# Mixture-of-experts tail of a decoder block: groups gathered in one burst a pair later, 33 weight blocks asked ahead, the spill loop amid pair 14

## The chip, the cores and the metric

The kernel runs on one core of one Trainium2 chip, in one launch. Times are device microseconds (us). The core has TensorE (PE: matmuls, and PEld: weight loads of the array), VectorE (DVE), ScalarE (ACT), GpSimd (POOL) and SyncE (SP), which here issues DMAs. Tiles live in SBUF; matmuls write PSUM, of which the kernel uses eight banks.

## The reference

One layer for 512 tokens of width 1024, in float32: a gated linear attention and a block-sparse softmax attention in parallel, cross-attention into 256 memory tokens, and a mixture of experts (MoE). The change touches the MoE and what follows it:

```python
# top-1 of 4 groups, top-2 of 8 SwiGLU experts in the group: 1024 assignments over 32 experts
hid = silu(xb @ w_gate[e]) * (xb @ w_up[e])      # (.., 1024) -> (.., 512)
out[tok] += (hid @ w_down[e]) * w                # (.., 512) -> (.., 1024)
return rmsnorm(x + moe(rmsnorm(x, g_moe)), g_final)
```

Each of the 32 experts has 6.29 MB of float32 weights, 201 MB together, and all of them are read.

## The kernel before

**Stages.** Up to about 500 us run the two attentions, the cross-attention and the router. The rest, which is about half of the time, is the MoE in 16 pairs of experts (`for p in range(NP)`), and then the final norm and the stores.

**Slots.** Every expert has 64 slots (`CAP`). A token's two assignments become integer codes (expert number times 512, plus rank in the expert). A group is four experts, that is two pairs: `group_hots` (L1187) compares the codes with the group's 256 slots on VectorE and leaves a one-hot tile `oh`; `gather` (L1195) multiplies the tokens' high and low halves with it on TensorE, eight steps of eight matmuls of 256 columns, and ScalarE copies each step's PSUM bank into `xT`. Group 0 is gathered during the routing (`c_gather`, L1037), the last part of it just ahead of pair 0.

**One pair.** `gate_up` (L1219): eight steps `k` of eight PE instructions into two PSUM banks `gu`; `hidden` (L1225): Silu on ScalarE, product on VectorE; `hidden_t` (L1232): transposes on TensorE and a copy on ScalarE; `down` (L1240): four steps `ft` into `y_ps`; `rows_hilo` splits that. While ScalarE and VectorE make the hidden values, TensorE runs fillers: steps of the generator `comb`, which puts the pair before back on its tokens (`c_ps`, added to `x` on VectorE), and steps of `gat`, the gather of the next group. Before, a group's gather starts in the even pair and takes four steps there and four in the odd pair after it, for pairs two and three further on; its `oh` is made at the end of the odd pair ahead.

**Weights.** `load_pairs` (L953) lists the loads of 512 KB: for each pair 16 of gate and up (L940, in four rounds of four), then 8 of down (L946). So load 24 p is the first of pair p. `eload(n)` (L966) asks for loads up to number n on SP's queue. Each takes a tile of the pool `bp`, of `NB` = 48 tiles, and waits on SP until the tile's last reader is done; tiles come back in the order in which they were let go. The pool also holds `x` (4 tiles), the tokens' halves `xrh` and `xrl` (8), the broadcast weights `wts` (1), `xT` (2 for each group that is alive) and `oh` (1). `DEPTH` = 30 says how many loads beyond the pair's first are asked for at its start; `D0` says it for pair 0. The DMA completions are counted on eight semaphores, and a load waits until the one eight before it has landed.

**Codes spread.** `c_bcast` (L1066) turns codes and weights so that every partition holds all of them: four steps, each of four transposes on TensorE and a copy on ScalarE, for two rows of codes and two of weights. `slot_rows` (L1205) reads them on VectorE for each pair. Before, the four steps stand in pair 0, at k = 2 to 5.

**Spill loop.** Assignments beyond an expert's 64 slots would be done by `overflow` (L1265), a loop with a run-time count; with these inputs the count is zero. Its entry reads the count into a register of each engine (L1266), and all engines meet twice (L1268). Before, it stands ahead of pair 15. `elimit` holds the loads back at 368 until it is passed (`12 * (NE - 2) + SPILL_AT`).

**End.** `finish` (L1385) scales and stores each 128-token tile in two halves of 256 KB (L1388, L1390), all eight stores on SP's queue.

Of the kernel before, what the change touches and what calls it, by code (L numbers as in the profile page):

```python
# [21 lines left out]
P = 128  # L22
T = 512
# [3 lines left out]
NE = 32  # L27
CAP = 64
# [42 lines left out]
def block_kernel(ctx, tc, x, mem, g_mem, rel_bias, g_mix, w_in, w_alpha_up, b_alpha, g_gla_head, w_proj_gla,  # L71
# [3 lines left out]
    nc = tc.nc  # L75
# [25 lines left out]
    def ps(name, shape, parts=P):  # L101
        return pp.tile([parts] + list(shape), F32, tag="p", name=name)
# [54 lines left out]
    def drain(*gens):  # L157
        for g in gens:
            for _ in g:
                pass  # L160
# [775 lines left out]
    def load_gate_up(e, to=None):  # L936

        for i, (q, w) in enumerate((q, w) for q in range(4) for w in (w_exp_gate, w_exp_up)):
            b = to[i % len(to)] if to else blk("we", [2, 512])
            SY.dma_start(b, wexp(w, e, 2 * q, 2 * q + 2))  # L940
            yield b
# [6 lines left out]


    blocks = [[] for _ in range(NE)]  # L950
    eloads, elimit = [0], [12 * (NE - 2) + SPILL_AT]

    def load_pairs():  # L953
        for p in range(NE // 2):
# [77 lines left out]
    def c_gather_part(t, kk, q):  # L1032
        for a in range(2):
            mm(g0[kk][:, a, :], (xrh, xrl)[q][t][:, tcol(2 * kk + a)], oh[:, t, :], t == 0 and a == 0 and q == 0,
               t == NT - 1 and q == 1, skip_group_check=True)
# [19 lines left out]
    def c_weights():  # L1055
        V.tensor_tensor(ge, gl, bc(gm, [NT, 4]), op=ALU.subtract)
        V.tensor_tensor(ex, m2, m1, op=ALU.subtract)
        S.activation(ge, ge, AF.Exp)
        S.activation(ex, ex, AF.Exp)
        V.tensor_reduce(gs, ge, axis=AX.X, op=ALU.add)  # L1060
        V.scalar_tensor_tensor(den, ex, 1.0, gs, op0=ALU.add, op1=ALU.mult)
        V.reciprocal(wts[:, :, 0:1], den)
        V.tensor_tensor(wts[:, :, 1:2], wts[:, :, 0:1], ex, op=ALU.mult)
        V.tensor_scalar(sid, e512, pslot, None, op0=ALU.add)
# [76 lines left out]
    c_low(NT - 1)  # L1141
    for kk in range(KD // 2):
        c_gather_part(NT - 1, kk, 0)
    c_weights()
    c_gather(NT - 1)
    S.activation(small("warm", [1]), neghalf[:, 0:1], AF.Silu)
# [45 lines left out]
            tile_hots(oh, rel, t, 4 * CAP)  # L1192
        return oh

    def gather(oh, xT, ns):  # L1195

        for k in range(KD):
            o = ps("g_ps", [ns])
            for t in range(NT):
                for q, src in enumerate((xrh, xrl)):  # L1200
                    mm(o, src[t][:, tcol(k)], oh[:, t, :], t == 0 and q == 0, t == NT - 1 and q == 1)
            S.activation(xT[k], o, AF.Copy, scale=gfeat[:, k:k + 1])
            yield
# [21 lines left out]
    def hidden(gu, ws, n=P, hid=None):  # L1225
        hid = (med("hid", [4, P]) if hid is None else hid)[0:n]
        row = hid.rearrange("p a b -> p (a b)")
        S.activation(row, gu[0][0:n], AF.Silu)  # L1228
        V.scalar_tensor_tensor(row, row, ws[:, 0:1], gu[1][0:n], op0=ALU.mult, op1=ALU.mult)  # L1229
        return hid  # L1230

    def hidden_t(hid, n=P):  # L1232
        t_ps = ps("ht_ps", [4, n])
        for a in range(4):
            PE.transpose(t_ps[:, a, :], hid[:, a, :], ident[0:n, 0:n])  # L1235
        hid_t = med("hid_t", [4, n])
        S.activation(hid_t, t_ps, AF.Copy)
        return hid_t
# [13 lines left out]
        for i in range(2):  # L1252
            mm(o, ot[:, tcol(t)], y[i], first and i == 0, i == 1)

    def combine(ot, ys):

        for t in range(NT):
            for c, y in ys.items():
                o = ps("c_ps", [512])
                product(o, ot, t, y)  # L1260
                xs = x_sb[t][:, 512 * c:512 * c + 512]
                V.tensor_tensor(xs, o, xs, op=ALU.add)  # L1262
                yield t, c

    def overflow(xi, xb):  # L1265
        n_extra = nc.values_load(xi[0:1, 0:1], min_val=0, max_val=NX - 1,  # L1266
                                 skip_runtime_bounds_check_because="2 T assignments fill fewer than NX whole blocks")
        with tc.For_i(0, n_extra, 1, iteration_sync='staggered') as i:  # L1268
            e = nc.sync.value_load(xi[0:1, bass.ds(i + 1, 1)], min_val=0, max_val=NE - 1)
            base = small("base", [1])  # L1270
            V.tensor_copy(base, xb[:, bass.ds(i, 1)])
            rel = small("relx", [NT, 2])
            V.tensor_scalar(rel, code, base, None, op0=ALU.subtract)
            codes = small("codes", [1])
            V.tensor_tensor(codes, pslot, base, op=ALU.add)
            take, take2 = cut(blk("loop", [D])), cut(blk("loop2", [D]))
            oh, part, oa = blk("oh", [NT, CAP], F32R), take([CAP]), take([T])
            xT, hid = take2([KD, CAP]), take2([4, P])
            xT = [xT[:, k, :] for k in range(KD)]
            for t in range(NT):  # L1280
                tile_hots(oh, rel, t, CAP, part)
            drain(gather(oh, xT, CAP))
            ot, ws = slot_rows(codes[0:CAP], CAP, oa)
            to = [blk("we", [2, 512]) for q in range(4)]
            gu, load = [ps("gu_ps", [512]) for q in range(2)], load_gate_up(bass.ds(e, 1), to)
            for j in range(4):
                w = list(islice(load, 2))
                for k in (2 * j, 2 * j + 1):
                    gate_up(gu, k, xT[k:k + 1], [{2 * j + q: w[q] for q in range(2)}])
            hid_t = hidden_t(hidden(gu, ws, CAP, hid), CAP)  # L1290
            y_ps, load = [ps("y_ps", [512]) for c in range(2)], load_down(bass.ds(e, 1), to)
            for ft in range(4):
                down(y_ps, hid_t, ft, [{8 + ft: next(load)}])
            parts = med("yh", [512], F32R), med("yl", [512], F32R)
            for c in range(2):
                drain(combine(ot, {c: rows_hilo(y_ps[c], CAP, parts)}))

    NP = NE // 2
    bcast, slot, spill = c_bcast(), None, spill_list()
    comb, gat = iter(()), iter(())  # L1300
    xT_next = None
    for p in range(NP):
        w = blocks[2 * p:2 * p + 2]
        used = 24 * p
        if p == NP - 1:
            eload(elimit[0])
            overflow(*spilled)
            elimit[0] = 12 * NE
        eload(used + D0[0] if p == 0 else used + DEPTH)
        if p % 2 == 0 and p:  # L1310
            xT = xT_next
        gu = [ps("gu_ps", [512]) for q in range(2)]
        s0 = (p % 2) * P
        for k in range(KD):
            gate_up(gu, k, [xT[k][:, s0 + CAP * i:s0 + CAP * i + CAP] for i in range(2)], w)
            if k % 2:
                eload(D0[1 + k // 2] if p == 0 else used + DEPTH + 2 * (k + 1))
            if p == 0 and k >= BC_AT:
                next(bcast, None)
                if k == BC_AT + 3:  # L1320
                    slot = slot_rows(sid[:, 0:1])
                    oh_next = group_hots(1)
        if p % 2 == 0 and p + 2 < NP:
            xT_next = rows2("xT", KD, 4 * CAP)
            gat = gather(oh_next, xT_next, 4 * CAP)
        if p == NP - 1:
            gf = blk("gf", [D])
            SY.dma_start(gf, bcast_rows(g_final, D))
        hid = hidden(gu, slot[1])
        gs = 4 if p + 2 < NP else 0  # L1330
        steps(gat, min(gs, 1))
        steps(comb, 2 if gs else 4)
        hid_t = hidden_t(hid)
        for i in range(3):
            steps(gat, min(gs, 1))
            steps(comb, 2)
        drain(comb)
        ot = slot[0]
        if p + 1 < NP:
            slot = slot_rows(sid[:, 2 * p + 2:2 * p + 3])  # L1340
        if p % 2 and p + 3 < NP:
            oh_next = group_hots((p + 3) // 2)
        if p >= 2:
            next(spill, None)
        y_ps = [ps("y_ps", [512]) for c in range(2)]
        if p == NP - 1:
            break
        for ft in range(4):
            down(y_ps, hid_t, ft, w)
            eload(used + DEPTH + 16 + 2 * (ft + 1))  # L1350
        ys = {c: rows_hilo(y_ps[c]) for c in range(2)}
        comb = combine(ot, ys)


# [30 lines left out]
    def finish(t, r):  # L1385
        o = blk("xo", [512])
        V.scalar_tensor_tensor(o, x_half(t, 1), r, gf[:, 512:1024], op0=ALU.mult, op1=ALU.mult)  # L1387
        SY.dma_start(out[tcol(t), 512:1024], o)  # L1388
        S.activation(xg[t], xg[t], AF.Copy, scale=r)
        SY.dma_start(out[tcol(t), 0:512], xg[t])  # L1390

    part = [last_products(c) for c in range(2)]
    for ft in range(4):
# [15 lines left out]
            finish(t - 1, r[t - 1])  # L1409


SPILL_AT = 8
MEM_AT, WOS = (0, 1), {5: 4, 6: 4}
LATE = [], [], range(4)
BC_AT = 2
# [2 lines left out]
QW = (0, 3, 4, 4)  # L1418
NB = 48
WARM = (14, 12)  # L1420
DEPTH = 30
D0 = 34, 37, 41, 44, 47
AHEAD, SAHEAD = 4, 2
FILL = (4, 3), (5, 3), (5, 4), (5, 4)
MANUAL = None
# [28 lines left out]
```

## Time and profile before

| | us |
|---|---|
| median of 3 runs (985.02 to 985.25) | 985.21 |
| the profiled execution | 985.1 |
| its span, first to last instruction | 983.3 |
| PE busy | 961.1 (98%) |
| VectorE busy | 474.8 (48%) |
| ScalarE busy | 311.7 (32%) |
| bytes moved by DMA | 252.52 MB |

The 1.8 us between span and time lie around the span. In the profile's slices, each of the 40 digits stands for 24.6 us; a PE that is always busy may still be waiting inside its matmuls. A timeline row gives start, duration, engine, line, operation, tiles and the count of merged instructions, and in brackets idle time before it and what ended it. A row of SP is the issue of a DMA, not its transfer.

### The profile page before, as it was taken

What the parts mean: (1) busy time and instruction counts of PE and PEld (TensorE: products, weight loads), DVE (VectorE), ACT (ScalarE), POOL (GpSimd) and SP (SyncE); (2) the same over time, 40 slices, a digit from 0 to 9 for tenths busy, and PEclk for the clock granted to TensorE, in tenths of its full rate; (3) what the DMA queues carried; (4) which work ended last, traced back from release to release, by engine and by line L of the source; (5) the groups of instructions that cost most, each with busy time, mean ns of one, the idle gap of its engine ahead of it and who ended that gap; (6) DMA issues with size and microseconds to landing.
All of it is one profiled execution on the core that took longest, in us unless ns stands there. A gap on an engine that the chain in (4) does not pass through costs nothing. (4 is left out here: it accounts for less than half of the span.)

```text
span 983.3 us, 13899 instructions
## 1 busy us (share of the span) xinstructions
PE 961.1 (98%) x5305; PEld 645.5 (66%) x5305; DVE 474.8 (48%) x1048; ACT 311.7 (32%) x631; POOL 32.7 (3%) x46
## 2 busy tenths in 40 slices
PE   9999999999999999999999999999999999999985
PEld 7889779888788888999844555544555554455432
DVE  6343863345555746566752543434453333444314
ACT  5452633445446424455521111111111111111003
POOL 3200010000000000000000000000000000000003
PEclk9999999999999999999999999999999999999998
DMA  9512347133133522644588999999999999999993
GB/s 300 160 44 58 71 65 193 44 86 86 60 133 129 176 81 67 198 190 196 200 331 329 409 408 409 409 409 408 409 409 409 409 408 409 409 409 409 409 383 148
DMA packets 117161, 252.52 MB, mean 257 GB/s; under 512 B 10310, under 2 KB 61795, under 8 KB 117092
## 3 DMA queue, kind: packets, MB, share of 16 engines
q1 hardware_dynamic: 117092, 251.60, 69.3%
q8 instruction: 43, 0.70, 0.3%
q14 instruction: 26, 0.21, 0.1%
HBM read 247.90 MB, written 3.67 MB: 256 GB/s over the span
## 5 line engine op out<-in xcount | busy, mean ns | idle before, releaser
L136 PE MATMUL gu_ps<-we,xT 128*64 128x512 f32 x1024 | 229.3, 597 | 5.1 <-PEq L1268 3.8
L136 PEld LDWEIGHTS gu_ps<-we,xT 128*64 128x64 f32 x1024 | 78.0, 138 | 150.5 <-issue 134.6
L213 DVE TENSOR_TENSOR wlo<-wraw,whi 128x1024 fp32r<-128x1024 f32 (+1 forms) x71 | 86.6, 1238 | 90.0 <-ACT whi L212 89.8
L136 PE MATMUL y_ps<-we,hid_t 128*64 128x512 f32 x512 | 114.2, 595 | 0.3 <-issue 0.3
L1229 DVE SCALAR_TENSOR_TENSOR hid<-hid,ws,gu_ps 128x512 f32<-128x512 f32 x16 | 11.9, 747 | 194.9 <-PE gu_ps L136 194.9
L1262 DVE TENSOR_TENSOR x<-c_ps,x 128x512 f32<-128x512 f32 x120 | 76.7, 685 | 38.9 <-PE c_ps L136 38.9
L131 PE MATMUL fo<-hTh,whi 128*128 128x512 f32 x224 | 90.5, 404 | 0.0
L133 PE MATMUL fo<-hTh,wlo 128*128 128x512 f32 x224 | 87.5, 391 | 0.0
L132 PE MATMUL fo<-hTl,whi 128*128 128x512 f32 x224 | 87.4, 390 | 0.0
L136 PEld LDWEIGHTS y_ps<-we,hid_t 128*64 128x64 f32 x512 | 36.3, 137 | 68.8 <-issue 55.7
L212 ACT ACTIVATE whi<-wraw 128x1024 fp32r<-128x1024 f32 (+2 forms) x73 | 74.5, 1043 | 1.9 <-DMA wraw<-in_w_in_dram 1.8
L1228 ACT ACTIVATE hid<-gu_ps 128x512 f32<-128x512 f32 x16 | 9.6, 597 | 197.5 <-PE gu_ps L136 197.5
L136 PE MATMUL g_ps<-oh,xrh 128*128 128x256 f32 x256 | 64.6, 293 | 1.7 <-DVE oh L1030 1.7
L136 PE MATMUL g_ps<-oh,xrl 128*128 128x256 f32 x256 | 61.6, 281 | 0.0
L136 PEld LDWEIGHTS g_ps<-oh,xrh 128*128 128x128 f32 x256 | 47.0, 189 | 14.9 <-PE gu_ps L136 9.7
L133 PE MATMUL ro<-whi,hTl 128*128 128x256 f32 (+1 forms) x192 | 55.4, 289 | 0.8 <-DVE hTl L333 0.8
L131 PE MATMUL ro<-whi,hTh 128*128 128x256 f32 (+1 forms) x192 | 56.0, 291 | 0.0
L132 PE MATMUL ro<-wlo,hTh 128*128 128x256 f32 (+1 forms) x192 | 55.5, 289 | 0.2 <-POOL wlo L213 0.2
L212 ACT ACTIVATE yh<-y_ps 128x512 fp32r<-128x512 f32 x32 | 19.1, 598 | 109.9 <-PE y_ps L136 109.9
L136 PE MATMUL c_ps<-yh,ot 128*128 128x512 f32 x128 | 50.8, 397 | 0.7 <-ACT yh L212 0.7
L136 PE MATMUL c_ps<-yl,ot 128*128 128x512 f32 x128 | 50.8, 397 | 0.2 <-DVE yl L213 0.2
L131 PEld LDWEIGHTS fo<-hTh,whi 128*128 128x128 f32 x224 | 42.0, 188 | 12.0 <-issue 3.9
(320 smaller groups left out, 1544.5 us busy)
## 6 DMA issues: line engine op xcount, KB each, us to landing
we<-in_w_exp_gate_dram SPq DMA_DIRECT2D x128, 512.0 KB, 10.2
we<-in_w_exp_up_dram SPq DMA_DIRECT2D x128, 512.0 KB, 10.2
we<-in_w_exp_down_dram SPq DMA_DIRECT2D x128, 512.0 KB, 10.2
wraw<-in_w_in_dram SPq DMA_DIRECT2D x38, 512.0 KB, 3.8
wraw<-in_w_out_dram SPq DMA_DIRECT2D x8, 512.0 KB, 6.1
wraw<-in_w_ckv_dram SPq DMA_DIRECT2D x8, 512.0 KB, 4.6
wraw<-in_w_proj_gla_dram SPq DMA_DIRECT2D x4, 512.0 KB, 3.9
wraw<-in_w_proj_moba_dram SPq DMA_DIRECT2D x4, 512.0 KB, 4.3
```

Of the source, the lines that this page charges most:

```text
L131: PE.matmul(o, lh, rh, start=first, stop=False)
L132: PE.matmul(o, lh, rl, start=False, stop=False)
L133: PE.matmul(o, ll, rh, start=False, stop=last)
L136: PE.matmul(o, l, r, start=first, stop=last, **kw)
L212: S.activation(hi, src, AF.Copy)
L213: eng.tensor_tensor(lo, src, f(hi), op=ALU.subtract)
L1228: S.activation(row, gu[0][0:n], AF.Silu)
L1229: V.scalar_tensor_tensor(row, row, ws[:, 0:1], gu[1][0:n], op0=ALU.mult, op1=ALU.mult)
L1262: V.tensor_tensor(xs, o, xs, op=ALU.add)
```

## The change

- `gather` of a group and its `oh` move into the odd pair just ahead of the group: `oh` is made at k = 3 of that pair, and all eight steps run between its gate/up and its down stage, two steps in each of four places (before: one in each of four places in two pairs). Even pairs have no gather steps.
- `DEPTH` is 33 (35 for pair 0) in place of 30 and the list `D0`.
- The spill loop stands in pair 14, ahead of k = 4, and `elimit` is 350 until then; its count is read into registers a pair earlier, and its PSUM tiles are taken as six banks of one name.
- The two steps of `c_bcast` for the codes run during the routing, ahead of `c_weights`; those for the weights at k = 2 and 3 of pair 0, and `slot_rows` follows at k = 3.
- The four stores L1390 are issued on ScalarE's queue.

```diff
-    eloads, elimit = [0], [12 * (NE - 2) + SPILL_AT]
+    eloads, elimit = [0], [SPILL[2]]
...
         c_gather_part(NT - 1, kk, 0)
+    bcast = c_bcast()
+    steps(bcast, 2)
     c_weights()
     c_gather(NT - 1)
...
-        if p == NP - 1:
-            eload(elimit[0])
-            overflow(*spilled)
-            elimit[0] = 12 * NE
-        eload(used + D0[0] if p == 0 else used + DEPTH)
+        depth = DEPTH[min(p, 1)]
+        if p == SPILL[0] - 1:
+            n_extra = nc.values_load(spilled[0][0:1, 0:1], min_val=0, max_val=NX - 1, skip_runtime_bounds_check_because=
+                                     "2 T assignments fill fewer than NX whole blocks")
+        eload(used + depth)
...
         for k in range(KD):
+            if (p, k) == SPILL[0:2]:
+                overflow(n_extra, *spilled)
+                elimit[0] = 12 * NE
             gate_up(gu, k, [xT[k][:, s0 + CAP * i:s0 + CAP * i + CAP] for i in range(2)], w)
             if k % 2:
-                eload(D0[1 + k // 2] if p == 0 else used + DEPTH + 2 * (k + 1))
+                eload(used + depth + 2 * (k + 1))
             if p == 0 and k >= BC_AT:
                 next(bcast, None)
-                if k == BC_AT + 3:
+                if k == BC_AT + 1:
                     slot = slot_rows(sid[:, 0:1])
-                    oh_next = group_hots(1)
-        if p % 2 == 0 and p + 2 < NP:
+            if p % 2 and p + 1 < NP and k == OH_AT:
+                oh_next = group_hots((p + 1) // 2)
+        if p % 2 and p + 1 < NP:
             xT_next = rows2("xT", KD, 4 * CAP)
             gat = gather(oh_next, xT_next, 4 * CAP)
...
-        gs = 4 if p + 2 < NP else 0
-        steps(gat, min(gs, 1))
-        steps(comb, 2 if gs else 4)
+        steps(gat, 2)
+        steps(comb, 2 if p % 2 and p + 1 < NP else 4)
         hid_t = hidden_t(hid)
         for i in range(3):
-            steps(gat, min(gs, 1))
+            steps(gat, 2)
             steps(comb, 2)
-        drain(comb)
+        drain(gat, comb)
...
-        if p % 2 and p + 3 < NP:
-            oh_next = group_hots((p + 3) // 2)
...
-        SY.dma_start(out[tcol(t), 0:512], xg[t])
+        S.dma_start(out[tcol(t), 0:512], xg[t])
...
-SPILL_AT = 8
+SPILL = 14, 4, 350
...
-DEPTH = 30
-D0 = 34, 37, 41, 44, 47
+DEPTH = 35, 33
+OH_AT = 3
```

## Rows read from the trace of the kernel before

**Rows 1.** The page's part 2, the span in 40 equal slices of 24.6 us: what the DMA engines moved.

```profile
GB/s 300 160 44 58 71 65 193 44 86 86 60 133 129 176 81 67 198 190 196 200 331 329 409 408 409 409 409 408 409 409 409 409 408 409 409 409 409 409 383 148
```

**Rows 2.** The view of windows in four stretches: length in us, busy time of PE, PEld, DVE, ACT and POOL with the number of their instructions, granted clock of TensorE, busy share of the DMA engines, GB/s.

```profile
500.00:520.00 20.00, 19.52 (x97) 7.89 (x98) 9.79 (x26) 6.27 (x12) 0.00 (x0) 1.00 0.94 349
520.00:541.00 21.00, 21.00 (x109) 8.59 (x109) 3.12 (x8) 2.83 (x6) 0.00 (x0) 1.00 0.85 326
541.00:561.00 20.00, 20.00 (x110) 10.96 (x108) 13.13 (x27) 4.30 (x8) 0.00 (x0) 1.00 1.03 408
561.00:900.00 339.00, 338.19 (x1733) 166.53 (x1730) 136.54 (x277) 49.87 (x93) 0.00 (x0) 1.00 1.03 409
```

**Rows 3.** The view of waits for SP's queue: line, what it waited for, us in total, times, longest. The first two rows are of the stretch from 499 to 541 us, the last of that from 541 to 900 us.

```profile
SPq L946 <- PE y_ps L136: 7.1, 1, 7.1
SPq L946 <- PE gu_ps L136: 6.4, 2, 3.6
...
SPq L940 <- DMA we<-in_w_exp_down_dram: 78.9, 89, 1.5
```

**Rows 4.** SP's timeline: loads of gate and up (L940) and of down (L946), around pair 0, and around pairs 14 and 15; last, from the page's part 6, the median time from issue to landing of such a load, and of the earlier stages' loads of the same size.

```profile
492.08 0.33 SPq L940 DMA_DIRECT2D we<-in_w_exp_up_dram  x1
499.79 0.33 SPq L940 DMA_DIRECT2D we<-in_w_exp_gate_dram  x1
...
507.77 16.89 SPq L946 DMA_DIRECT2D we<-in_w_exp_down_dram  x8
...
541.20 9.58 SPq L946 DMA_DIRECT2D we<-in_w_exp_down_dram  x8
...
909.46 0.33 SPq L940 DMA_DIRECT2D we<-in_w_exp_gate_dram  x1
...
912.01 9.25 SPq L946 DMA_DIRECT2D we<-in_w_exp_down_dram  x8
...
931.21 0.33 SPq L940 DMA_DIRECT2D we<-in_w_exp_up_dram  x1
938.72 0.33 SPq L940 DMA_DIRECT2D we<-in_w_exp_gate_dram  x1
...
943.76 9.16 SPq L946 DMA_DIRECT2D we<-in_w_exp_down_dram  x8
...
we<-in_w_exp_gate_dram SPq DMA_DIRECT2D x128, 512.0 KB, 10.2
...
wraw<-in_w_in_dram SPq DMA_DIRECT2D x38, 512.0 KB, 3.8
```

**Rows 5.** PE's timeline. The first five rows are of a pair with four gather steps, from its gate/up to the next pair's; the last two are the first matmuls of pair 14, which has none, and those of pair 15.

```profile
818.67 13.90 PE L136 MATMUL gu_ps<-we,xT 128*64 128x512 f32 x64
...
836.80 0.28 PE L136 MATMUL g_ps<-oh,xrh 128*128 128x256 f32 x1
...
837.75 0.39 PE L136 MATMUL c_ps<-yh,ot 128*128 128x512 f32 x1
...
838.68 0.28 PE L136 MATMUL g_ps<-oh,xrh 128*128 128x256 f32 x1
...
847.56 14.64 PE L136 MATMUL gu_ps<-we,xT 128*64 128x512 f32 x64
...
907.90 11.32 PE L136 MATMUL gu_ps<-we,xT 128*64 128x512 f32 x50
...
938.86 16.50 PE L136 MATMUL gu_ps<-we,xT 128*64 128x512 f32 x64 [3.77 <-PEq L1268]
```

**Rows 6.** Pair 0: PE's timeline from the last matmuls of gate/up to down, and VectorE's row for the hidden values.

```profile
513.12 3.65 PE L136 MATMUL gu_ps<-we,xT 128*64 128x512 f32 x16
...
518.93 0.66 PE L1235 MATMUL ht_ps<-keep,hid 128*128 128x128 f32 x4 [0.16 <-DVE hid L1229]
...
522.38 7.09 PE L136 MATMUL y_ps<-we,hid_t 128*64 128x512 f32 x32
...
518.13 0.74 DVE L1229 SCALAR_TENSOR_TENSOR hid<-hid,ws,gu_ps 128x512 f32<-128x512 f32 x1
```

**Rows 7.** Around the start of pair 0: ScalarE's copies of the last gathered part into xT, and the first step of the spread codes, on TensorE and on ScalarE.

```profile
499.39 1.55 ACT L1047 ACTIVATE xT<-g_ps,gfeat 128x256 f32<-128x256 f32 x4
...
505.20 0.65 PE L1073 MATMUL cb_ps<-keep,rt_code 128*128 128x128 f32 x4
...
505.88 0.60 ACT L1074 ACTIVATE codes<-cb_ps 128x512 int16<-128x512 f32 x1 [3.43 <-PE cb_ps L1073]
```

**Rows 8.** The instructions of line L1268, the meeting of the engines at the spill loop, on three queues: count, duration in ns, first and last start.

```profile
L1268 SPq EVENT_SEMAPHORE  x28: 17/17/17, 932.1 to 938.6; - x28
L1268 PEldq EVENT_SEMAPHORE  x8: 51/51/51, 931.8 to 938.6; - x8
...
L1268 DVEq EVENT_SEMAPHORE  x8: 21/21/21, 936.6 to 938.6; - x8
```

**Rows 9.** The stores' first half: its scaling on ScalarE and its four issues on SP (ns min/median/max, first and last start); last, GB/s in 40 slices of the stretch from 900 to 984 us (2.1 us each).

```profile
L1389 ACT ACTIVATE xg<-xg,rr x4: 706/714/722, 974.7 to 977.2; 128x512 f32<-128x512 f32 x4
L1390 SPq DMA_DIRECT2D out_dram<-xg x4: 383/494/607, 975.9 to 979.3; - x4
...
GB/s 408 414 398 410 412 408 412 408 410 412 410 410 410 406 412 404 412 343 287 334 384 373 412 414 416 417 412 408 410 291 10 0 0 0 0 4 251 380 368 0
```

More of the change, by code (lines that the diff above doesn't have):

```diff
@@ L1193, in group_hots, with gather @@
         return oh
-    def gather(oh, xT, ns):
+    def gather(oh, xT, ns, to=None):
         for k in range(KD):
-            o = ps("g_ps", [ns])
+            o = to[k % 2] if to else ps("g_ps", [ns])
             for t in range(NT):
@@ L1230, in hidden, with hidden_t @@
         return hid
-    def hidden_t(hid, n=P):
-        t_ps = ps("ht_ps", [4, n])
+    def hidden_t(hid, n=P, t_ps=None):
+        t_ps = ps("ht_ps", [4, n]) if t_ps is None else t_ps
         for a in range(4):
@@ L1253, in product, with combine @@
             mm(o, ot[:, tcol(t)], y[i], first and i == 0, i == 1)
-    def combine(ot, ys):
+    def combine(ot, ys, to=None):
         for t in range(NT):
             for c, y in ys.items():
-                o = ps("c_ps", [512])
+                o = to[t] if to else ps("c_ps", [512])
                 product(o, ot, t, y)
@@ L1263, in combine, with overflow @@
                 yield t, c
-    def overflow(xi, xb):
-        n_extra = nc.values_load(xi[0:1, 0:1], min_val=0, max_val=NX - 1,
-                                 skip_runtime_bounds_check_because="2 T assignments fill fewer than NX whole blocks")
+    def overflow(n_extra, xi, xb):
         with tc.For_i(0, n_extra, 1, iteration_sync='staggered') as i:
@@ L1281, in overflow @@
                 tile_hots(oh, rel, t, CAP, part)
-            drain(gather(oh, xT, CAP))
+            pb = [ps("sp_ps", [512]) for q in range(6)]
+            drain(gather(oh, xT, CAP, [b[:, 0:CAP] for b in pb[0:2]]))
             ot, ws = slot_rows(codes[0:CAP], CAP, oa)
             to = [blk("we", [2, 512]) for q in range(4)]
-            gu, load = [ps("gu_ps", [512]) for q in range(2)], load_gate_up(bass.ds(e, 1), to)
+            gu, load = pb[2:4], load_gate_up(bass.ds(e, 1), to)
             for j in range(4):
@@ L1289, in overflow @@
                     gate_up(gu, k, xT[k:k + 1], [{2 * j + q: w[q] for q in range(2)}])
-            hid_t = hidden_t(hidden(gu, ws, CAP, hid), CAP)
-            y_ps, load = [ps("y_ps", [512]) for c in range(2)], load_down(bass.ds(e, 1), to)
+            hid_t = hidden_t(hidden(gu, ws, CAP, hid), CAP, pb[4][:, 0:4 * CAP].rearrange("p (a n) -> p a n", a=4))
+            y_ps, load = pb[0:2], load_down(bass.ds(e, 1), to)
             for ft in range(4):
@@ L1295, in overflow @@
             for c in range(2):
-                drain(combine(ot, {c: rows_hilo(y_ps[c], CAP, parts)}))
+                drain(combine(ot, {c: rows_hilo(y_ps[c], CAP, parts)}, pb[2:6]))
     NP = NE // 2
-    bcast, slot, spill = c_bcast(), None, spill_list()
+    slot, spill = None, spill_list()
     comb, gat = iter(()), iter(())
-    xT_next = None
     for p in range(NP):
@@ L1349, in block_kernel @@
             down(y_ps, hid_t, ft, w)
-            eload(used + DEPTH + 16 + 2 * (ft + 1))
+            eload(used + depth + 16 + 2 * (ft + 1))
         ys = {c: rows_hilo(y_ps[c]) for c in range(2)}
```

## The prediction

> **What bounds the kernel now.** I read first what the DMA engines moved, by slices: from 541 us on they stand at 408 to 409 GB/s until the end of the MoE, and in the two slices before that at 331 and 329 [rows 1]; the windows put the change of level at 541 [rows 2]. Then SP's queue. Its pattern of 16 gate and up and 8 down loads for each pair lets a reader count: the down loads that begin at 541.20 are those of pair 2 (numbers 64 to 71), those at 912.01 are pair 14's (352 to 359) [rows 4]. So 288 loads were issued in 370.81 us, 1.29 us for each, 30.9 for a pair of 24. TensorE needs less: 28.9 from pair 11's first matmul to pair 12's (847.56 - 818.67) [rows 5]. The transfers are the slower of the two by 2.0 us a pair; TensorE uses up the lead that the loads had, and at the end its gate/up stage is stretched (16.50 in pair 15 for 13.90) [rows 5]. A PE that is busy for 98% of the span hides this.
>
> The end hangs on the last load: it is issued at 943.76 + 9.16 - 0.33 = 952.6 and lands 10.2 later, at 962.8 [rows 4]; the rest of pair 15, the norm and the stores take 20.5 us to the span's end at 983.3.
>
> What can be won is time in which the transfers were held back. Load 32 goes out at 499.79 on an idle queue (the one before went at 492.08) and lands some 3.8 later, like a single load of the earlier stages: 503.6. Load 64 lands at 541.20 + 10.2 = 551.4 [rows 4]. Without a break it would land at 503.6 + 32 x 1.29 = 544.9, so 6.5 us were lost. The waits of SP say to what: until 541 to TensorE, for tiles that are still being read (one wait of 7.1 for down, 6.4 for gate/up of pair 0), after that mostly to the landing of earlier loads [rows 3].
>
> **The change, part by part.** The profiled execution took 985.1, its span 983.3 and 1.8 around it; it is within 0.1 of the median, and the sum is made against it.
>
> Tiles. Of 48, others hold x 4, halves 8, spread weights 1, xT 4 and oh 1: 30 are left for loads. After the change only one group is alive, and oh only inside the odd pair, where it can take the tile that the old xT gives back at k = 3: 33 are left. A load waits for the reader of the load 33 before it, and no longer for one 30 or 31 before: two or more loads earlier in TensorE's order, 2 x 1.29 = 2.6 us.
>
> Codes spread sooner. ScalarE begins to copy the last gathered part to xT at 499.39, and TensorE starts pair 0 half a us later. Two steps are put ahead of that: each 0.65 on TensorE and 0.60 on ScalarE [rows 7]. I take 1.5 later (0 if they fall into waits, 2.5 if nothing overlaps): pair 0 starts at 501.4. Its gate/up is rid of two steps, 1.2 to 1.3, and ends within 0.3 of before.
>
> Pair 0, middle. Before, VectorE makes group 1's one-hot tile ahead of the hidden values, which begin only at 518.13, and down starts at 522.38 [rows 6]. Now only the chain is left, from the end of gate/up at 516.8: Silu 0.6 (a like copy took 0.60 [rows 7]), product 0.74, transposes 0.66, copy 0.6. Down starts at about 519.2, 3.2 earlier, and pair 1 at 526.2. No filler covers these 2.6 us, but four gather steps (0.95 each: 837.75 - 836.80 [rows 5]) no longer stand there.
>
> Pairs. An even pair takes 28.9 - 3.8 = 25.1, an odd one 32.7. Pairs 1 to 13 are seven odd and six even: 379.5, so TensorE would reach pair 14 at 905.7, with about 1 us of waits for loads at 906.7 (before: 907.90 [rows 5]). Fillers stay long enough: ahead of the transposes an even pair has eight c_ps matmuls (838.68 - 837.75 = 0.93 for four, so 1.9), an odd one four of them and 1.9 of gather, against a chain of 1.4.
>
> Early transfers. Load 32 waits for the last part of group 0's gather, so it moves 1.5 later and lands at 505.1. Without any break load 64 would land at 546.4, 5.0 sooner than before. The least is 2.6 - 1.5 = 1.1, if only the tiles count. The waits for pair 0's gate/up stay; the long one for its down goes, since down comes 3.2 sooner and is needed two loads later. I take 3.0 (1.1 to 5.0). What could be late next is pair 1, where 11.8 us pass between gate/up and down (4.2 without gather, 7.6 of gather) and give no tile back; eight loads in flight cover 10.3 of them. After that TensorE's lead on the loads' order grows by 2.0 a pair, and the transfers run without a break.
>
> Spill loop. Before, SP issues nothing between 931.21 and 938.72, 7.5 us. Load 367 lands at 941.4; 16 more at 1.29 would end at 962.0, and they end at 962.8 [rows 4]: it cost 0.8. VectorE comes last to the loop, at 936.6, and TensorE starts again at 938.86, 2.3 later; its queue had been there at 931.8, while its matmuls ran until 938.86 - 3.77 = 935.1, 3.3 ahead [rows 5, 8]. After, VectorE and ScalarE are done with pair 13 about 2 us into pair 14, the register reads are a pair earlier, and TensorE's queue comes to k = 4 at 906.7 + 6.9 - 3.3 = 910.3. The loop is over at 912.6, before the queued matmuls run out. SP stops ahead of load 350, whose turn would be 909.46 - 3.0 = 906.5: 6.1 us, a bit less than before. I count no difference (-0.8 if it is free, +3 if TensorE's queue isn't ahead there and SP waits for 9.4 us).
>
> Stores. ScalarE's four scalings and issues would take 4 x (0.71 + 0.49) from 974.7, until 979.5; before the last issue ended at 979.3 + 0.6 = 979.9. The slices show 380 and 368 GB/s there, close to the 409 that the loads reach [rows 9]. I take half of the difference, -0.2 (-0.9 to +0.3).
>
> The Trainium skill says in "DMA: Bandwidth & Descriptors", section "Issuing engines are not separate DMA queues", that DMAs of all engines run on the same 16 DMA engines, and that a second issuer saves only the time that its sequencer takes. By that rule the stores would win at most their issue time, and with the engines nearly full nothing: the sum would be 982.1 with it and 981.7 by the issue times alone. No run so far shows ScalarE issuing.
>
> Sum: -3.0 + 0 - 0.2 = -3.2; 985.1 - 3.2 = 981.9. TensorE alone would be done with pair 15 earlier, so the last load's landing (about 959.8) still sets the end.
>
> **The rivals.** (1) The spread is hidden in waits: pair 0 starts at 499.9, everything is 1.5 sooner, 980.4. For it: VectorE and ScalarE both idle there; against: ScalarE works in order, and the spread stands ahead of the copies. (2) The loop holds SP longer: TensorE's queue is stopped by a load that hasn't landed and isn't 3.3 ahead. 2.5 more, 984.4. For it: pair 14's loads were just in time before. (3) The change doesn't do what it says: oh and the new xT fill the pool, and loads stay 31 ahead. Only pair 0's earlier down is left, 1.0 + 0.2: 983.9. (4) Slower. In an odd pair the pool is full (33 + 15 tiles); the second half of the new xT can only take oh's tile, which is free when the last gather matmul is done. ScalarE stands at the fifth copy until then, four PSUM banks of eight stay taken, and TensorE waits for a bank. Pair 14 then comes later by seven times that idle time, less the 1 us that it waits anyway, and since load 350 stands behind the loop in pair 14, the transfers come later too. 1 us in each odd pair: 981.9 + 6 = 987.9; from 0.9 on it is slower than before by over 0.2%. Against it: with four banks taken, the other four still serve c_ps, which VectorE empties in time before.
>
> **How the numbers follow.** About 0.2% (2 us) is what a measurement of this kernel can tell from no change; faster is under 983.2, slower over 987.2. Forecast 0.50 (its own range 980.5 to 983.4), rival 1 0.12, rival 2 0.15, rival 3 0.11, rival 4 0.12. Faster: nearly all of the forecast and rival 1, 0.60; same: rivals 2 and 3 with the forecast's edge, 0.27; slower: rival 4 and the worst of the loop, 0.13. From the bounds above and the rivals the range is 979.7 to 985.6; beyond it are rival 4 and the last few per cent of rivals 1 and 2.
>
> **What would show it.** Down of pair 0 starts near 519, pair 0 near 501.4. GB/s is above 380 already from 505 to 541, and load 64 lands near 548. Odd pairs take 32.7, even ones 25.1, until about pair 12, with no idle in front of g_ps or c_ps. TensorE has no gap at L1268; SP's pause ahead of load 350 is about 6 us. The last load lands near 960. Wrong would be: SP still waiting for y_ps for several us after 520, g_ps idle in odd pairs, a gap of TensorE in pair 14, or a last landing at 962 or later.

## The result and the profile after

The changed kernel takes 1001.22 us, the median of 6 runs (993.83 to 1003.41), against 985.52 for the kernel before in the same comparison (985.02 to 986.52): a ratio of 1.0148, 95% interval 1.0114 to 1.0181. It is slower by 15.7 us where 3.2 faster were forecast, and far outside the range. The profiled execution took 1002.59, its span 1000.8, so 17.5 more than the span before.

The page's row of GB/s, to be held against [rows 1], and windows in the stretches of [rows 2], with the same columns; the last goes to the end of the loop in pair 14:

```profile
GB/s 299 153 45 62 67 72 179 65 63 85 64 170 130 201 6 148 115 316 103 252 366 409 364 409 399 410 409 409 409 409 409 409 408 409 409 408 234 266 410 145
...
500.00:520.00 20.00, 18.04 (x89) 6.47 (x89) 8.67 (x24) 5.77 (x13) 0.00 (x0) 1.00 0.91 347
520.00:541.00 21.00, 21.00 (x106) 7.91 (x103) 5.41 (x13) 2.18 (x4) 0.00 (x0) 1.00 1.03 409
541.00:561.00 20.00, 18.43 (x102) 12.72 (x103) 8.07 (x15) 3.69 (x9) 0.00 (x0) 0.91 0.90 351
561.00:900.00 339.00, 331.17 (x1634) 158.75 (x1632) 132.85 (x274) 44.84 (x86) 0.00 (x0) 0.97 1.03 408
900.00:931.00 31.00, 31.00 (x174) 17.19 (x172) 12.84 (x25) 6.20 (x12) 0.00 (x0) 1.00 0.50 198
```

The early transfers came: 409 from 520 to 541 us, where the kernel before moved 326. Three things are new. From 541 to 561 the transfers fall to 351 (408 before), while TensorE idles for 1.6. From 561 to 900 TensorE idles for 7.8 of the 339 us (0.8 before), at a mean granted clock of 0.97 for 1.00. And the transfers fall to half between 900 and 931.

Where TensorE idles is read from pair 1's timeline: PE's rows ahead of its down stage, then ScalarE's, then VectorE's, and last a wait of SP from 525 to 562 us (start, duration, in brackets the idle time before it and what ended it):

```profile
547.19 0.28 PE L136 MATMUL g_ps<-oh,xrh 128*128 128x256 f32 x1
547.31 0.28 PE L136 MATMUL g_ps<-oh,xrl 128*128 128x256 f32 x1
547.43 0.40 PE L136 MATMUL c_ps<-yh,ot 128*128 128x512 f32 x1
547.66 0.40 PE L136 MATMUL c_ps<-yl,ot 128*128 128x512 f32 x1
548.84 0.50 PE L136 MATMUL c_ps<-yh,ot 128*128 128x512 f32 x1 [0.78 <-DVE x L1264]
549.17 0.40 PE L136 MATMUL c_ps<-yl,ot 128*128 128x512 f32 x1
550.35 0.41 PE L136 MATMUL g_ps<-oh,xrh 128*128 128x256 f32 x1 [0.78 <-DVE x L1264]
550.58 0.40 PE L136 MATMUL g_ps<-oh,xrl 128*128 128x256 f32 x1
...
551.21 0.41 PE L136 MATMUL g_ps<-oh,xrh 128*128 128x256 f32 x1
551.42 0.41 PE L136 MATMUL g_ps<-oh,xrl 128*128 128x256 f32 x1
...
553.55 0.41 PE L136 MATMUL g_ps<-oh,xrl 128*128 128x256 f32 x1
...
554.90 7.09 PE L136 MATMUL y_ps<-we,hid_t 128*64 128x512 f32 x32
...
544.79 0.48 ACT L1204 ACTIVATE xT<-g_ps,gfeat 128x256 f32<-128x256 f32 x1 [0.48 <-PE g_ps L136]
554.00 1.57 ACT L1204 ACTIVATE xT<-g_ps,gfeat 128x256 f32<-128x256 f32 x4 [8.73 <-PE g_ps L136]
...
548.09 0.69 DVE L1264 TENSOR_TENSOR x<-c_ps,x 128x512 f32<-128x512 f32 x1 [1.54 <-PE c_ps L136]
549.61 0.69 DVE L1264 TENSOR_TENSOR x<-c_ps,x 128x512 f32<-128x512 f32 x1 [0.82 <-PE c_ps L136]
...
SPq L940 <- PE y_ps L136: 10.4, 4, 8.1
```

Four things stand here. The fifth copy into xT waits 8.7 us, until the last gather matmul is done: rival 4's place exactly. TensorE has two gaps of 0.78, each ended by VectorE's add of the product just before: a product that ends at 548.06 is added from 548.09 to 548.78, and only then TensorE goes on. After the second gap the gather matmuls follow each other by 0.21 us, where earlier in the pair it is 0.12. And pair 1's down stage, which gives the next tiles back, begins only at 554.90, so SP waits 8.1 for one tile; that is where the transfers fall to 351.

The waits of PE show that it is so in each of the six odd pairs from 1 to 11 (us in total, times, longest), and windows put the matmuls behind the gaps on the lower of the two clock levels, 1.2 GHz for 2.4:

```profile
PE c_ps L136 <- DVE x L1264: 4.7, 6, 0.8
PE g_ps L136 <- DVE x L1264: 4.7, 6, 0.8
...
540.00:548.00 8.00, 8.00 (x59) 7.23 (x57) 2.84 (x5) 2.50 (x5) 0.00 (x0) 1.00 1.03 409
550.30:553.80 3.50, 3.45 (x17) 3.45 (x18) 0.00 (x0) 0.00 (x0) 0.00 (x0) 0.54 1.03 410
```

An odd pair takes 36.35 (pair 1 begins at 525.47, pair 2 at 561.82), not the forecast 32.7; an even one 25.1 to 25.2, as forecast. Pair 13 has the same burst with no gap at all, and takes 32.7 (894.14 to 926.87); its last loads are held back by the limit of 350. So six pairs lose 3.65 each.

What that does to the end is seen at line L1268, to be read against [rows 8], and in SP's loads 349 and 350 around it; the last row is TensorE's start of pair 14:

```profile
L1268 SPq EVENT_SEMAPHORE  x28: 17/17/17, 908.4 to 931.6; - x28
L1268 PEldq EVENT_SEMAPHORE  x8: 51/51/51, 929.5 to 931.6; - x8
...
908.08 0.33 SPq L940 DMA_DIRECT2D we<-in_w_exp_up_dram  x1
931.75 0.33 SPq L940 DMA_DIRECT2D we<-in_w_exp_gate_dram  x1
...
926.87 14.54 PE L136 MATMUL gu_ps<-we,xT 128*64 128x512 f32 x64
```

SP stood at the loop from 908.4 to 931.6, since TensorE reached pair 14 at 926.87, 20.2 later than the forecast's 906.7. Load 350 goes out at 931.75, the last load lands near 980.2 (it was to land at 959.8), and pair 15's gate/up is stretched to 20.3 us by waits for loads.

### The profile page after: what moved, and what is told of

It reads as the page before. It is cut to its first block, busy times and chain, and to the rows that moved or that the text cites. A ratio compares the mean times of both kernels' runs of the same rounds, so it can differ in the third digit from the quotient of the medians.

```text
span 1000.8 us, 13916 instructions
## 1 busy us (share of the span) xinstructions
PE 969.0 (97%) x5305; PEld 648.5 (65%) x5305; DVE 474.1 (47%) x1048; ACT 309.5 (31%) x631; POOL 32.7 (3%) x46
## 4 chain that ended last, share of the span: by engine, by line
PE 90%; DMA 4%; DVE 2%; ACT 2%; issue 1%; SPq 0%; POOL 0%; POOLq 0%; ACTq 0%; DVEq 0%
PE gu_ps L136 20%; PE y_ps L136 11%; PE fo L131 8%; PE fo L133 8%; PE fo L132 8%; PE g_ps L136 7%; PE c_ps L136 6%; PE ro L133 3%; PE ro L131 3%; PE ro L132 3%; DMA we<-in_w_exp_up_dram 3%; PE x2o L136 2%; PE xo L132 1%; PE xo L133 1%; PE xo L131 1%; PE mo_ps L136 1%
## 5 line engine op out<-in xcount | busy, mean ns | idle before, releaser
L136 PE MATMUL gu_ps<-we,xT 128*64 128x512 f32 x1024 | 226.1, 593 | 4.2 <-DMA we<-in_w_exp_gate_dram 3.1
L136 PEld LDWEIGHTS gu_ps<-we,xT 128*64 128x64 f32 x1024 | 73.5, 137 | 152.2 <-issue 129.1
L136 PE MATMUL g_ps<-oh,xrh 128*128 128x256 f32 x256 | 70.6, 314 | 6.1 <-DVE x L1264 4.7
L136 PE MATMUL g_ps<-oh,xrl 128*128 128x256 f32 x256 | 68.8, 307 | 0.0
L136 PEld LDWEIGHTS g_ps<-oh,xrh 128*128 128x128 f32 x256 | 53.2, 213 | 15.0 <-issue 7.3
L136 PE MATMUL c_ps<-yh,ot 128*128 128x512 f32 x128 | 53.0, 414 | 5.4 <-DVE x L1264 4.7
L136 PEld LDWEIGHTS g_ps<-oh,xrl 128*128 128x128 f32 x256 | 53.7, 215 | 0.4
## 6 DMA issues: line engine op xcount, KB each, us to landing
we<-in_w_exp_gate_dram SPq DMA_DIRECT2D x128, 512.0 KB, 10.2
we<-in_w_exp_down_dram SPq DMA_DIRECT2D x128, 512.0 KB, 10.2
```

Of the source, the lines that this page charges most:

```text
L136: PE.matmul(o, l, r, start=first, stop=last, **kw)
```

## The experiments

Twelve kernels ran. The theories have letters: A (the full pool: ScalarE waits for the one-hot tile and keeps PSUM banks), B (the burst is too much for ScalarE and VectorE), C (the limit of 350 is the main loss), and, from the second set on, D (which tile is given which bank).

**One load fewer.** In the changed kernel:

```diff
-DEPTH = 35, 33
+DEPTH = 35, 32
```

> The changed kernel with one load fewer asked ahead (32 in place of 33, nothing else). Theory A (full pool): in the odd pairs the second half of the new xT no longer has to take the one-hot tile's place, ScalarE's fifth xT copy follows its matmuls within 1 us (8.7 in the changed kernel), TensorE has no idle in front of c_ps and g_ps, odd pairs take 32.7 us in place of 36.35, pair 14 begins at about 907 and the time is 982 to 985. Theory B (the burst itself: eight gather steps and four c_ps products in one pair are more than ScalarE and VectorE can clear from eight PSUM banks): odd pairs stay at 36 us, the idle of 0.8 us stays, the time stays near 1001.

999.39 us (998.23 to 999.99), ratio to before 1.0133 (1.0116 to 1.0150). Neither theory held as put. Pair 1 and pair 3 of this run: ScalarE's fifth copy, PE's rows of the two gaps, and windows of both pairs:

```profile
546.61 0.47 ACT L1204 ACTIVATE xT<-g_ps,gfeat 128x256 f32<-128x256 f32 x1 [1.40 <-PE g_ps L136]
...
548.78 0.50 PE L136 MATMUL c_ps<-yh,ot 128*128 128x512 f32 x1 [0.78 <-DVE x L1264]
...
550.29 0.39 PE L136 MATMUL g_ps<-oh,xrh 128*128 128x256 f32 x1 [0.78 <-DVE x L1264]
...
525.00:561.00 36.00, 34.44 (x188) 18.05 (x186) 14.05 (x28) 7.15 (x14) 0.00 (x0) 1.00 1.00 393
...
587.00:623.00 36.00, 34.44 (x180) 18.84 (x178) 14.38 (x38) 6.19 (x12) 0.00 (x0) 0.95 1.02 403
```

ScalarE's long wait is gone, as A says, and both gaps stand where they were, as long as before. So the gaps don't come from the wait for the tile. Each looks like one bank used by two tiles in a row: the add of a product has to be over before the next product may begin. The run also splits the loss. Pair 1 keeps its clock and takes 34.85 from its gate/up to pair 2's (525.41 to 560.25); pair 3 has the same gaps and a mean clock of 0.95, and takes 36.35 (585.43 to 621.78). With 32.7 for a pair without gaps (shown below), the gaps cost 2.1 and the clock 1.5.

**The limit at 368**, with 33 and with 32 loads ahead, and with 33 in even pairs and 32 in odd ones:

```diff
-SPILL = 14, 4, 350
+SPILL = 14, 4, 368
```

> The changed kernel with the loads held at 368 in place of 350 until the loop in pair 14 is passed. Theory A: the stall of the odd pairs alone makes TensorE late, in all seven odd pairs now (in pair 13 the held loads had left tiles free): pair 14 begins at 926.9 + 3.6 = 930.5, no load is late after it, pair 15 begins 25.2 later, its down stage 18.1 after that, and the end is 23.7 behind that: 997.5, a time near 999 (1002.6 for the changed kernel's profiled execution). Theory C (the limit of 350 is the main loss, since SP stood at the loop from 908.4 to 931.6): 985 to 988.

> Both edits: 32 loads ahead and the limit at 368. Theory A: no stall in the odd pairs, and SP comes to load 368 only after TensorE has passed the loop, so the transfers don't pause there at all: 409 GB/s until the last load; 0 to 1 us under the run with 32 ahead alone, 981 to 984. Theory B: near 1000, like the changed kernel. If SP's pause ahead of load 350 costs more than the loads in flight cover, the difference to the run with 32 ahead alone is 2 us or more.

> 33 loads ahead in even pairs and 32 in odd ones (34 in pair 1's count is not reached; pair 0 keeps 35), limit 368. Theory A: when the burst runs, as many tiles are taken as with 32 ahead throughout, so no stall; the 33rd load of the even pairs is worth at most 1.3 us at the start: 980.5 to 984, within 1.3 of the run with 32 throughout. Theory B: near 1000.

997.02 (995.46 to 998.70), 998.28 (995.48 to 1000.25) and 997.09 (996.55 to 997.54), ratios 1.0108, 1.0133 and 1.0113. The first is near theory A's 999 and far from C's 985 to 988: with the loads free, pair 13 has its gaps too, pair 14 begins at 930.5, as expected, and pair 15's down stage at 973.8, as worked out; it shows what late pairs cost, not yet why they are late. It also prices the limit: from pair 14's start to the end of the span it is 66.4 here and 73.9 in the changed kernel, so with late pairs 7.5 us at the end come from the loads held behind the loop. The other two show again that a tile to spare cures nothing; in them all seven odd pairs keep their gaps.

**Which tile has which bank.** The built program lists the bank of each PSUM tile. For pair 3 of the changed kernel and of the run that follows, and for pair 13 of the changed kernel and of the run with the limit at 368, in TensorE's order (g: a gather step; c: a product; t: the transposes; the number is the bank):

```
changed, 3    g2 g6  c4 c0  t5  g3 g7  c1 c4  g0 g1  c4 c4  g4 g2  c6 c5
early, 3      g2 g7  c3 c1  t6  g0 g5  c4 c2  g7 g3  c1 c6  g0 g5  c4 c2
changed, 13   g3 g6  c4 c0  t5  g7 g2  c1 c3  g6 g4  c0 c5  g7 g2  c1 c3
368, 13       g3 g6  c4 c0  t5  g7 g2  c1 c4  g0 g1  c4 c4  g4 g3  c6 c5
```

In pair 3 of the changed kernel the fifth and sixth product and the seventh gather step are all given bank 4: the two gaps stand in front of the second and the third of them. Pair 13 tells the same: no bank twice in a row and no gap in the changed kernel, three times bank 4 and both gaps with 368. As I read the built program, a bank is given when the program is built, in the order in which the build sees tiles come back; there, the copies into xT stand behind the pair's last loads, since the tiles of xT are asked for after them, so their banks come back late and one bank goes round among what is left. That reason is a reading and was not shown. With 32 loads ahead the list has the same three in a row. Whether the bank plan makes the gaps was put to the test by asking for the tiles of xT earlier:

```diff
                 oh_next = group_hots((p + 1) // 2)
+                xT_next = rows2("xT", KD, 4 * CAP)
+                for h in (0, KD // 2):
+                    G.memset(xT_next[h][:, 0:1], 0.0)
         if p % 2 and p + 1 < NP:
-            xT_next = rows2("xT", KD, 4 * CAP)
```

> The changed kernel with one edit: the new xT's two tiles are taken at k = 3 of the odd pair, next to the one-hot tile, by writing one column of each on GpSimd (a column that the gather writes over). Loads stay 33 ahead, the limit stays 350. When the kernel is built, the copies into xT then no longer stand behind the pair's last loads, and the eight PSUM banks come round in turn (without it, two c_ps products and a gather step in a row are given one bank). Theory D (bank plan): the two gaps of 0.78 us in front of c_ps and g_ps go, the clock stays at 1.00 in the odd pairs, which take 32.7 us; pair 14 begins near 907 and the time is 981 to 984. Theory B (the burst is more than ScalarE and VectorE can clear): gaps stay, 36 us, 998 to 1002.

982.69 us (981.22 to 983.89, 7 runs), ratio 0.9972 (0.9961 to 0.9984): theory D's number. TensorE in pair 1, without a gap, and at pair 14; the window of pair 1; then line L1268:

```profile
547.34 0.40 PE L136 MATMUL c_ps<-yh,ot 128*128 128x512 f32 x1
547.57 0.40 PE L136 MATMUL c_ps<-yl,ot 128*128 128x512 f32 x1
547.81 0.39 PE L136 MATMUL c_ps<-yh,ot 128*128 128x512 f32 x1
...
907.02 13.90 PE L136 MATMUL gu_ps<-we,xT 128*64 128x512 f32 x64
...
525.00:561.00 36.00, 36.00 (x198) 18.87 (x196) 14.66 (x29) 7.23 (x14) 0.20 (x2) 1.00 1.03 406
...
L1268 SPq EVENT_SEMAPHORE  x28: 17/17/17, 903.9 to 911.8; - x28
L1268 PEldq EVENT_SEMAPHORE  x8: 51/51/51, 909.6 to 911.8; - x8
```

Pair 1 takes 32.7 (525.4 to 558.1). The accounts close: six pairs lose 3.65 in the changed kernel, 21.9; here pair 13 waits 2.0 for loads (its gate/up takes 15.9 for 13.9), which the late TensorE of the changed kernel never did; the difference is 19.9, and that is what lies between the spans (1000.8 and 980.9).

**Two banks for the products**, which leaves the tiles, the 33 loads and ScalarE's wait as they are in the changed kernel:

```diff
-                o = to[t] if to else ps("c_ps", [512])
+                o = to[t] if to else cbank[c] if cbank else ps("c_ps", [512])
...
             gat = gather(oh_next, xT_next, 4 * CAP)
+            cbank.extend(ps("c_ps", [512]) for c in range(2))
...
         drain(gat, comb)
+        cbank.clear()
```

> The changed kernel with one edit: in a pair with a burst the eight c_ps products take turns on two PSUM banks of their own, in place of whatever bank the build gives each. The tiles are as in the changed kernel: 33 loads ahead, and the fifth xT copy still waits for the one-hot tile until the last gather matmul is done. Theory D (bank plan alone): that wait of ScalarE stays at 8 us or so and costs TensorE nothing; no gap in front of c_ps and g_ps, clock 1.00, odd pairs 32.7 to 33, 981 to 985. Theory A (the full pool is a cause of its own): TensorE still waits in the odd pairs, over 34 us each, and the time is over 990.

982.79 us (981.70 to 985.70), ratio 0.9976 (0.9963 to 0.9990). ScalarE in pair 1, and windows of pair 1 and of the pairs after it:

```profile
551.14 1.57 ACT L1204 ACTIVATE xT<-g_ps,gfeat 128x256 f32<-128x256 f32 x4 [5.19 <-PE g_ps L136]
...
525.00:561.00 36.00, 36.00 (x198) 18.80 (x195) 14.66 (x29) 7.06 (x14) 0.00 (x0) 1.00 1.03 408
561.00:900.00 339.00, 338.02 (x1735) 164.56 (x1732) 138.45 (x286) 48.18 (x93) 0.00 (x0) 1.00 1.03 409
```

ScalarE still stands at the fifth copy until the burst is over (5.2 us and not the expected 8, since the burst is shorter by the 3.6 that the gaps and the clock had cost), and it costs TensorE nothing: no gap, and pair 1 takes 32.7 (526.15 to 558.88). This is the run that separates the two causes, since only the bank plan differs. Theory A falls, D stands.

**The loop and the limit, with the early tiles.** The limit at 368; the loop ahead of pair 15 (`SPILL = 15, 0, 368`); the limit at 354:

> As the run with the early tiles, and the loads held at 368 in place of 350 until the loop in pair 14. Theory D: odd pairs 32.7 us; SP doesn't stop ahead of load 350, and TensorE has passed the loop before load 368 has its turn: 409 GB/s throughout from 541 us on. If SP's pause of about 6 us is covered by the loads in flight, the time is within 0.8 of the run with 350; if not, up to 5 us under it: 977 to 983. Theory B: 995 to 999, as without the early tiles.

> Early tiles, loads held at 368, and the spill loop ahead of pair 15 as in the kernel before. My own term: the loop's place is worth nothing between -0.8 and +3 us against pair 14. With the loop ahead of pair 15, SP stops at load 368 until TensorE gets there (some 7 us, 0.8 of it lost in the kernel before): 0.5 to 3 us slower than the run with the loop in pair 14 and 368. Rival: TensorE pays for the loop itself, since the transfers are ahead by then: 3.8 us (its idle at the loop in the kernel before) slower.

> Early tiles and the loads held at 354 until the loop. In the run with 350, SP stood for 8.3 us (903.6 to 911.9) while TensorE's queue came to the loop at 909.6; in the run with 368, TensorE stood for 15.5 us while SP came to it at 927.7. Four more loads of 1.28 bring SP there at 908.7, just ahead of TensorE: neither waits long. The transfers lose no more than 0.5 us in place of 3.0 (load 383 landed at 960.3; without a break 957.3): 979.5 to 981, 2 to 3 us under the run with 350. If the pause was covered by the loads in flight: no difference.

With 368: 993.72 (993.57 to 995.28), ratio 1.0087, a miss by more than 10 us. The window from 910 to 930, TensorE's wait and SP's arrival tell why:

```profile
910.00:930.00 20.00, 5.05 (x24) 1.44 (x20) 0.00 (x0) 0.00 (x0) 0.00 (x0) 0.68 1.03 410
...
PE gu_ps L136 <- PEq L1268: 15.5, 1, 15.5
...
L1268 SPq EVENT_SEMAPHORE  x28: 17/17/17, 927.7 to 930.3; - x28
L1268 PEldq EVENT_SEMAPHORE  x8: 51/51/51, 910.6 to 930.3; - x8
```

I had counted only SP's wait for TensorE. All engines meet at the loop, and SP comes there when it has issued every load up to the limit, at its 1.28 us each: at 927.7. TensorE waited for SP. In the runs with 368 and a late TensorE this did not show. With the loop ahead of pair 15: 983.79 (982.90 to 984.73), ratio 0.9984 (0.9974 to 0.9993); TensorE waits 3.1 there, near the rival's 3.8. Its comparison with 368 is void; it is 1.8 over the run with 354, and the two runs' times just touch (982.90 in both). With 354, SP comes to the loop at 910.0 and TensorE's queue at 910.8, as intended; the transfers go on at 407 GB/s from 900 to 930 (370 with 350), but the time is 981.98 (980.47 to 982.90), ratio 0.9963 (0.9951 to 0.9975): 0.7 under the run with 350 where 2 to 3 were expected, and not told apart from it.

**Stores, depth, spread**, each with the early tiles (the stores with 368, the others with 354):

> Early tiles, limit 368, and all eight stores on SP's queue again. My own term for the stores: 0.2 us slower than with half of them on ScalarE's queue (0.9 slower to 0.3 faster). Rival: no difference at all, since the tail of 13.8 us from the last y_ps matmul to the end is the same in the kernel before and in the changed one.

> As the run with 354, and 34 loads ahead in place of 33. In the odd pairs one load then waits for the one-hot tile; ScalarE and TensorE don't, since their tiles are taken before. A load less late at the start, where SP still waits for readers until pair 1: at best 1.3 us under the run with 354. Rival: no difference, since transfers run without a break from 505 us on as it is.

> As the run with 354, and the four steps that spread codes and weights in pair 0 again, as in the kernel before. My own term: the spread ahead of pair 0 costs 1.5 us at its start (0 to 2.5), which its gate/up wins back, while the loads that wait for pair 0 are later by the 1.5. So undone: first load of pair 0's start about 1 us earlier, down of pair 0 later since slot_rows ends two steps later (hidden values wait for it); 0 to 1.5 us faster, or up to 2 slower if load 48 and on, which wait for pair 0's down, come later.

All stores on SP: 994.51 (993.79 to 995.07) against 993.72, not told apart; the tail from the last y_ps matmul to the end is 13.8 us in the kernel before, in the changed one and in the run with early tiles. 34 loads ahead: 981.21 (980.88 to 981.59), the fastest of all, ratio 0.9956 (0.9944 to 0.9969), 4 us under the kernel before, but within the spread of the run with 33. Spread in pair 0 again: 981.51 (980.64 to 982.18), no difference that these runs show.

## Why the prediction was wrong

The step that failed is in **Pairs**: "an odd one 32.7". It holds for a pair whose PSUM banks come round in turn; in six of the seven odd pairs it was 36.35. I had checked that the fillers last long enough for the hidden values, and not which bank each filler gets: two products and a gather step in a row got one, and TensorE waited for VectorE in front of the second and the third, in the place where I had forecast no idle. That a bunched gather comes to such a plan because it holds more banks at a time than four steps in each of two pairs did is my reading, and no run shows it.

**Rival 4** named the place, the fifth copy, the wait for a bank and the way to the end over load 350; it had a chance of 0.12. Its mechanism was wrong: the runs with one load fewer and with two banks show that the full pool and ScalarE's wait cost nothing. My argument against it, that the other four banks still serve c_ps, holds in the run with two banks; in the changed kernel the tiles around the gaps had one bank between them. Its price of 1 us a pair was also short, by what no row of before showed: 2.1 for the two gaps (at each, matmuls start 1.18 apart, as at 547.66 and 548.84, where products follow each other by 0.23, and the start after it is 0.1 late too), and 1.5 more for matmuls at 1.2 GHz.

**The carry to the end** was as rival 4 put it: each late microsecond of TensorE came to the end, 19.9 of 19.9, because load 350 stands behind the loop. Without that it would have been fewer, but not none: by the 7.5 us that the run with 368 shows, some 12 of the 19.9 would have come through TensorE alone, an estimate.

The other terms can be read from the run with early tiles, which is the change without its bank plan: 982.69 for a forecast of 981.9. Point by point, forecast and run: pair 0 starts at 501.4 and 500.8; its down at 519.2 and 518.5; pair 1 at 526.2 and 525.4; an even pair 25.1 and 25.1 to 25.2; pair 14 at 906.7 and 907.0; the last load lands at 959.8 and near 960.3.

That the last landing came so close is in part luck, for two terms were off against each other. It is seen at loads 349 and 350: the first row is load 349 before, the others are both loads in the run with early tiles.

```profile
908.18 0.33 SPq L940 DMA_DIRECT2D we<-in_w_exp_up_dram  x1
...
903.58 0.33 SPq L940 DMA_DIRECT2D we<-in_w_exp_up_dram  x1
911.90 0.33 SPq L940 DMA_DIRECT2D we<-in_w_exp_gate_dram  x1
```

**Early transfers** were taken as 3.0 (1.1 to 5.0) and gave more: load 349, the last ahead of the loop, went out 4.6 earlier than before. Load 64 was already 3.9 earlier in the changed kernel (537.31 for 541.20). **The loop** was taken as no difference (-0.8 to +3) and cost 2.2 more than before: SP stood for 8.3 us where 6.1 were forecast, and the transfers lost 3.0 (load 349's 903.58 and 34 loads of 1.28 and 10.2 would be 957.3, and load 383 landed near 960.3), against the 0.8 of before. 4.6 less 2.2 is 2.4, which is what lies between the spans (983.3 and 980.9). **The stores** gave nothing that these runs can tell, where 0.2 was taken.

## What to carry to other kernels

When work is bunched, list for the busiest stretch which bank each PSUM tile gets, in the order of the engine that fills them: where one bank stands twice in a row, that engine can have to wait for the other one's whole instruction, though other banks are there (here 0.78 us at an add of 0.69). Asking for a later tile earlier can mend such a plan without moving any work. At a point where all engines meet, count the queue of every one of them up to it, the issuer of DMAs too: a limit that is too low stops the transfers, and one that is too high stops TensorE.

The Trainium skill says in "Perfetto Trace Analysis", section "Optimizing Tensor Performance", that independent groups of matmuls should go round through different banks, so that emptying one overlaps the next group. This case's traces agree: 0.78 of idle at each of the twelve places in the odd pairs of the changed kernel where the next tile had the same bank, none in the runs with early tiles and with two banks, where they went round.

## What the runs showed of the hardware

After two gaps of 0.78 us, 1.5 apart, in a stretch of TensorE that is otherwise full, the granted clock fell to its lower level, 1.2 GHz (0.54 in the window from 550.3 to 553.8). Not every time: with the same gaps pair 1 of the run with 32 loads ahead stayed at 1.00 and pair 3 fell to a mean of 0.95. What decides between them these runs don't show. In the run with two banks, which has no gaps, the mean from 561 to 900 stayed at 1.00. In the profiles of the five kernels with gaps, every odd pair that has them takes either 34.85 or 36.35 (to 0.03). The fall would account for the scatter of these kernels' times: 6 pairs by 1.5 us is 9.0, the changed kernel's times lie within 9.6, and its fastest execution (993.83) has a mean granted clock of 0.994 where the other five have 0.985 to 0.987. That is argued from these sums and was not tried by itself.

The Trainium skill's page "TensorE: Matmul & The Clock Gate", section "A second HAM failure mode: psum-queue depth-cycling", tells of a kernel that idles briefly between its groups of matmuls as it goes through the banks, and whose clock goes back and forth between its levels. The traces here agree, with the 0.54 above.

What stays open: why the build counts the copies into xT so late was read from the order of the built program, and only its cure was tried.
